# Attention issued in an order computed by a list scheduler, and the gate row applied after w_out

## The chip, the cores and the metric

One core of one Trainium2 chip runs the whole program. The metric is device time in microseconds, the median of the runs. Each core has a matrix engine (TensorE, PE), a vector engine (VectorE, DVE), a scalar engine (ScalarE, ACT), GpSimd (POOL) and a queue engine for transfers (SyncE, SP). Each engine runs its own instructions in the order in which they were issued to it and waits on semaphores for the others.

## What is computed

One transformer block on 1024 tokens of width 1024, batch 1, all in fp32. Cut to what matters here:

```
cond = silu(c)
sh1, sc1, gt1, sh2, sc2, gt2 = split(cond @ w_ada + b_ada, 6)      # "conditioning", 6 x 1024
h    = layer_norm(x) * (1 + sc1) + sh1
aq, ak, av, iq, ik, iw, gq, gk, gv, gr, glr, gate_a, gate_b = split(h @ w_in)
o_a  = sparse attention (8 heads of 64; per query the 256 best keys by an index score)
       logits = q.k / 8 + bias(distance);  p = softmax(logits);  o_a = p @ v
o_b  = gated linear attention, normed                              # 4 heads, 512 columns
merged = sigmoid(gate_a) * (o_a @ w_branch_a) + sigmoid(gate_b) * (o_b @ w_branch_b)
y    = merged @ w_out
x1   = layer_norm(2**0.25 * x + gt1 * y) * g1 + b1
h2   = layer_norm(x1) * (1 + sc2) + sh2
out  = layer_norm(2**0.25 * x1 + gt2 * mixture_of_experts(h2))     # 32 experts, 2 of them per token
```

## The kernel before

The program runs through stages: the first conditioning group (shift and scale 1) and the norm; the projections by w_in with index scores, top-k and the gated linear attention beside them; attention; branch a with the preparation of w_out; the products with w_out with the two norms and the routing; the experts; the last norm. Products that must be exact are made in three passes: an operand is split into a high part (a copy rounded by ACT) and a low part (the difference, by DVE or POOL), and `mm3` adds high x high, high x low and low x high.

**Attention** (lines 883 to 1003) goes by four pairs of heads `p`, each with eight blocks of 128 queries `i`. By the top-k, `acc[i]` already holds 0 or -1e30 per key. `scores(p, i)` lets POOL add mask and distance bias for the last 256 keys (`amb`), PE make the logits of both heads (`asp`, L904, contraction 64, each head on its half of the rows, n = 128(i+1) keys in chunks of at most 512, high and low parts of q and k in three passes), DVE add the mask and find the row's extreme in one custom operation (L908), ACT take the exponential with its row sum (L914), and DVE divide by the sum (L915, L916). Each head has a logits tile of its own, of four in all. `pv(p, u, P)`, for two query blocks at a time, transposes the shares by PE (`atp`, L932 and L933), copies them from PSUM by ACT or DVE in a fixed pattern (`DCOPY`, L936 and L938), multiplies by v (`aop`, L941, each head on its half of the columns), and splits the result into high and low parts (L944, L945). The values of one step are taken up after the scores of the next.

Between these steps `pump(FILL[u])` draws fillers from two generators: `ada_late`, the other two conditioning groups, and `branch_b`, the sixteen sums of o_b by w_branch_b (L124 to L126 by `mm3`, then L981 by DVE, which multiplies with the sigmoid of the gate). A conditioning group has eight steps of k; `ada_step` (L182 to L190) loads two tiles of 128x1024, half a megabyte each, and issues two matmuls on each (L189), each on 32 columns of the array:

```
for i in range(2):
    w = pool.tile([128, 1024], F32, name="wada", bufs=bufs)
    SY.dma_start(w, A["w_ada"][0, k * 128:(k + 1) * 128, c0:c0 + 1024])
    for q in range(2):
        PE.matmul(ps[32 * j:32 * j + 32], crep[:, k, :], w[:, q * 512:(q + 1) * 512], ...)
```

The first stage issues the same operation as four matmuls of 256 columns on one tile (L237). The attention stage stands outside of the manual schedules; the framework places its instructions, and the trace has them in an order that differs from the text (a conditioning step can stand between the transposes of one block).

**Branch a** (L1049 to L1084) goes by eight column blocks f: three-pass products of o_a with w_branch_a (`yps`), multiplied by gate a (L1064) and added to branch b (L1065) on DVE, then split (L1071 on ACT, L1072 on DVE) into `pg`. In the same loop a block of w_out is loaded, multiplied by the gate row gt1 (L1079, on POOL for the f in `GTP`, else on DVE, 128x512 at a time), and split (L1081 on ACT; L1082 on POOL for the f in `GTL`, else on DVE).

**The products** (L1381 to L1413) multiply the merged rows with w_out for each of eight tiles of 128 tokens, in four quarters; PSUM has five buffers `yps` for them and for transposes. `residual` (L1245) adds 2**0.25 x on DVE (L1248) and takes the statistics, and the norms, transposes, routing logits and routing of the tiles before are woven in. x tiles lie in five buffers `lx`.

Of the kernel before, what the change touches and what calls it, by code (L numbers as in the profile page):

```python
# [10 lines left out]
F32 = mybir.dt.float32  # L11
# [5 lines left out]
OP = mybir.AluOpType  # L17
# [39 lines left out]
GTL = (3, 7)  # L57
GTP = (0, 1, 2, 4, 5, 6)
FET = {0: 2, 4: 2, 5: 3, 6: 1, 7: 2}
FILL = (3, 2, 2, 1)  # L60
# [5 lines left out]
DCOPY = (1, 4)  # L66
ASB = 4
# [21 lines left out]
def _bucket_onehot():  # L89
# [8 lines left out]
    return np.ascontiguousarray(oh[:, ::-1])  # L98


@with_exitstack
def block_kernel(ctx, tc, A, out, dbg=None, stop=99):
# [78 lines left out]

    def ada_step(g, k, ps, pool, bufs):  # L182
        for i in range(2):
            w = pool.tile([128, 1024], F32, name="wada", bufs=bufs)
            c0 = g * 2048 + i * 1024
            SY.dma_start(w, A["w_ada"][0, k * 128:(k + 1) * 128, c0:c0 + 1024])
            for q in range(2):
                j = 2 * i + q
                PE.matmul(ps[32 * j:32 * j + 32], crep[:, k, :], w[:, q * 512:(q + 1) * 512],  # L189
                          start=(k == 0), stop=(k == KT - 1), tile_position=(0, 32 * j), skip_group_check=True)  # L190
# [581 lines left out]
    def load_pair(p):  # L772
        for f0, n in ((p * 128, "q"), (512 + p * 128, "k")):
            r = AP_[1].tile([128, S], F32, name="araw", bufs=2)
            SY.dma_start(r, dqk[f0:f0 + 128])
            hi, lo = pair_parts(p, n)
            SC.activation(hi, r, AF.Copy)
            GP.tensor_tensor(lo, r, hi.bitcast(F32), op=OP.subtract)

# [73 lines left out]
    fillers = []  # L853

    def pump(budget):
        while budget > 0 and fillers:
            try:
                budget -= next(fillers[0])
            except StopIteration:
                fillers.pop(0)  # L860

# [21 lines left out]
    def scores(p, i):  # L883

        n = (i + 1) * 128
        (qh, ql), (kh, kl) = QK[p, "q"], QK[p, "k"]
        tk = slice(i * 128, i * 128 + 128)
        f = max(0, n - 256)
        mbs, Ps, mxs = [], [], []
        for s in range(2):  # L890
            mb = apw.tile([128, 256], F32, name="amb")[:, :n - f]
            GP.tensor_tensor(mb, acc[i][:, f:], tb[:, 2 * p + s, 256 - (n - f):], op=OP.add)
            mbs.append(mb)
            Ps.append(apw.tile([128, S], F32, name="aP", bufs=8)[:, :n])
            mxs.append(small.tile([128, 5], F32, name="amx", bufs=8))
# [833 lines left out]
```

## Time and profile before

| | us |
|---|---|
| median of 3 runs (1466.23 to 1469.11) | 1466.5 |
| the profiled execution | 1464.93 |
| its span, first to last instruction | 1463.1 |
| PE busy | 1356.0 (93%) |
| DVE busy | 1166.0 (80%) |
| ACT busy | 729.3 (50%) |
| POOL busy | 499.9 (34%) |

The profile is one execution. The page has the busy time of each engine; the windows give it for a stretch of time, all or for one tile or line; the timeline lists instructions in order of time; the lines group instructions by line and shape. A busy PE is not one at its peak: matmuls are pipelined, so the step from one start to the next is the time that one costs, and the length shown with it is more.

### The profile page before, as it was taken

The page shows a single profiled execution, that of the slowest core. Times are in us where ns is not written, and L with a number is a line of the kernel's source. Part 1 is how long each engine was busy: PE and PEld are TensorE (multiplying, and loading weights), DVE is VectorE, ACT ScalarE, POOL GpSimd, SP SyncE. Part 2 cuts the span into 40 slices and gives each one's busy share as a digit, 9 for nine tenths or more (in the row PEclk, how much of TensorE's full clock was granted, in tenths as well). Part 3 has the DMA queues.
Part 4 walks back from the last instruction along what each step waited for, and adds up shares of the span by engine and source line. Part 5 has one row for each costly group of instructions (what it writes and reads, how often), then busy time and mean ns, then how long its engine had stood idle before and what let it go on. Part 6 is the DMA issues. An engine that isn't in the chain of part 4 may idle for free. (4 is left out here: it accounts for less than half of the span.)

```text
span 1463.1 us, 21360 instructions
## 1 busy us (share of the span) xinstructions
PE 1356.0 (93%) x7535; PEld 1058.7 (72%) x7535; DVE 1166.0 (80%) x2126; ACT 729.3 (50%) x1312; POOL 499.9 (34%) x502
## 2 busy tenths in 40 slices
PE   4988999999999999998999998799969999999975
PEld 2566788887888788983446666599957888888842
DVE  5649998988987899936656656867779999999957
ACT  2456775443243313125544543322327888888934
POOL 2466422374246422144334323521131222222114
PEclk9999999999999999999999999999968999999998
DMA  9454422112211232108555336766349999999965
GB/s 292 149 153 144 144 68 70 59 37 80 77 40 40 85 109 88 58 1 247 185 167 158 108 107 195 232 220 231 130 141 333 379 380 377 376 341 362 368 250 201
DMA packets 135679, 262.69 MB, mean 180 GB/s; under 512 B 20912, under 2 KB 71400, under 8 KB 135568
## 3 DMA queue, kind: packets, MB, share of 16 engines
q1 hardware_dynamic: 124112, 242.13, 48.4%
q0 software_dynamic: 9216, 16.80, 3.1%
q10 hardware_dynamic: 2240, 2.36, 0.5%
q8 instruction: 60, 0.98, 0.3%
q14 instruction: 51, 0.42, 0.1%
HBM read 229.61 MB, written 48.39 MB: 190 GB/s over the span
## 5 line engine op out<-in xcount | busy, mean ns | idle before, releaser
L1357 DVE TENSOR_TENSOR elo<-pg,ehi 128x1024 fp32r<-128x1024 f32 x188 | 219.1, 1220 | 17.5 <-ACT ehi L1352 9.3
L124 PE MATMUL pj<-hTh,whi 128*128 128x512 f32 (+1 forms) x528 | 210.9, 400 | 0.0
L125 PE MATMUL pj<-hTl,whi 128*128 128x512 f32 (+1 forms) x528 | 207.3, 393 | 1.9 <-DVE hTl L267 1.2
L126 PE MATMUL pj<-hTh,wlo 128*128 128x512 f32 (+1 forms) x528 | 207.2, 392 | 0.0
L1352 ACT ACTIVATE ehi<-pg 128x1024 fp32r<-128x1024 f32 x192 | 190.1, 1075 | 1.1 <-PE eph L126 1.1
L791 POOL TENSOR_TENSOR wlo<-raw,whi 128x512 fp32r<-128x512 f32 x84 | 111.8, 1344 | 207.3 <-ACT whi L790 196.3
L485 DVE MATCH_REPLACE8 acc<-m,acc 128x1024 f32<-128x1024 f32 (+2 forms) x192 | 167.4, 881 | 0.0
L482 DVE MAX8 m<-acc 128x8 f32<-128x1024 f32 (+2 forms) x192 | 162.6, 885 | 0.0
L464 DVE SCALAR_TENSOR_TENSOR acc<-ixr,iwt,acc 128x128 f32<-128x128 f32 (+3 forms) x120 | 127.2, 1115 | 13.9 <-ACT ixr L457 13.3
L124 PEld LDWEIGHTS pj<-hTh,whi 128*128 128x128 f32 (+1 forms) x528 | 98.7, 187 | 22.7 <-issue 1.7
L125 PEld LDWEIGHTS pj<-hTl,whi 128*128 128x128 f32 (+1 forms) x528 | 98.8, 187 | 22.5 <-DVE hTl L267 2.7
L126 PEld LDWEIGHTS pj<-hTh,wlo 128*128 128x128 f32 (+1 forms) x528 | 98.6, 187 | 22.8 <-issue 0.6
L124 PE MATMUL pj<-whi,hTh 128*128 128x256 f32 x384 | 111.8, 291 | 0.0
L125 PE MATMUL pj<-wlo,hTh 128*128 128x256 f32 x384 | 108.6, 283 | 0.0
L126 PE MATMUL pj<-whi,hTl 128*128 128x256 f32 x384 | 108.5, 283 | 0.0
L124 PE MATMUL eph<-ehi,xh 128*128 128x512 f32 x256 | 105.4, 412 | 0.0
L125 PE MATMUL eph<-elo,xh 128*128 128x512 f32 x256 | 102.7, 401 | 1.1 <-DVE elo L1362 1.1
L126 PE MATMUL eph<-ehi,xl 128*128 128x512 f32 x256 | 102.7, 401 | 0.0
L457 ACT ACTIVATE ixr<-ips 128x128 f32<-128x128 f32 (+7 forms) x128 | 80.3, 656 | 44.4 <-DVE acc L464 21.1
L1376 POOL DMA_INDIRECT xg<-dh,gidx x32 | 34.0, 1063 | 161.7 <-PE etp L1472 148.5
L124 PEld LDWEIGHTS pj<-whi,hTh 128*128 128x128 f32 x384 | 73.4, 191 | 6.9 <-issue 5.5
L124 PE MATMUL yps<-whi,pg 128*128 128x256 f32 x256 | 75.7, 296 | 2.2 <-ACT pg L1071 2.2
(322 smaller groups left out, 3272.1 us busy)
## 6 DMA issues: line engine op xcount, KB each, us to landing
pg<-in_w_exp_gate_dram SPq DMA_DIRECT2D x64, 512.0 KB
pg<-in_w_exp_up_dram SPq DMA_DIRECT2D x64, 512.0 KB
pg<-in_w_exp_down_dram SPq DMA_DIRECT2D x32, 1024.0 KB
wada<-in_w_ada_dram SPq DMA_DIRECT2D x48, 512.0 KB
raw<-in_w_in_dram SPq DMA_DIRECT2D x20, 1024.0 KB
sraw<-diq SPq DMA_DIRECT2D x68, 128.0 KB
dgate<-gate SPq DMA_DIRECT2D x32, 256.0 KB
gb<-dgate SPq DMA_DIRECT2D x32, 256.0 KB
```

What stands on the lines that cost most here:

```text
L124: PE.matmul(ps, ah, bh, start=first, stop=False)
L125: PE.matmul(ps, ah, bl, start=False, stop=False)
L126: PE.matmul(ps, al, bh, start=False, stop=last)
L457: SC.activation(r, ps, AF.Relu)
L464: V.scalar_tensor_tensor(acc[i], r, sc, acc[i], op0=OP.mult, op1=OP.add)
L482: V.max(m, acc[i])
L485: V.match_replace(acc[i], m, acc[i], -3.0e38)
L791: GP.tensor_tensor(lo[:, k:k + 2], raw[:, k:k + 2], hi[:, k:k + 2].bitcast(F32), op=OP.subtract)
L1352: SC.activation(h3, src, AF.Copy)
L1357: V.tensor_tensor(*args, op=OP.subtract)
L1376: GP.indirect_dma_start(out=x, out_offset=None, in_=dh2, in_offset=bass.IndirectOffsetOnAxis(ap=gi, axis=0), bounds_check=S - 1, oob_is_er ...
```

## The change

In attention a class `Order` takes every step of the stage with its engine (or a choice of ACT and DVE), a modelled time, the steps that it comes after, and the buffers that it takes and gives back. It is run when the program is built: again and again it takes, of the steps that may go, the one with the least start time plus a rank of its kind (`RANK`), and at the end emits all by start time, under a manual schedule for PE, ACT, DVE and POOL. A switch between kinds of PE work is modelled with 0.25 us, a megabyte of conditioning weights with 3.0 us and 2.0 us of lag.

The logits of both heads are one PSUM tile of two banks (`asp`, two of them) and one step. The copies from PSUM are made by ACT or DVE as the scheduler finds. A conditioning step loads 128x2048 at once and issues its four matmuls together. The eight bias loads of both groups are issued ahead of the order. Branch b's o_b parts lie in the conditioning's two buffers.

The gate row gt1 no longer multiplies w_out; `residual` multiplies the product with it on DVE. Of the low parts of w_out DVE makes those of the odd f, POOL those of the even f. `lx` has four buffers, and a tile `ly` is added.

```diff
-GTL = (3, 7)
-GTP = (0, 1, 2, 4, 5, 6)
+GTV = (1, 3, 5, 7)
-FILL = (3, 2, 2, 1)
+RANK = {"Q": 0.94, "R": -22.18, "E": 1.01, "N": 0.11, "T": 1.04, "C": -19.89, "A": 0.98, "H": -49.53, "L": -12.89, "D": 1.04,
+        "B": 0.96, "Z": -18.85, "Wh": 0.27, "Oh": 0.3, "Ol": -62.38, "pair": -3.46, "M": -1.4}
-DCOPY = (1, 4)
-ASB = 4
+class Order:
+    LATENCY, CHANGE = 0.15, 0.25
...
+    def start_of(self, name, free, done, mode):
+        engines, time, _, after, takes, _, m, rank, _ = self.todo[name]
+        if any(a not in done for a in after):
+            return None
+        at = max([done[a] for a in after], default=0.0)
+        for r in takes:
+            n = len(self.taken[r])
+            if n >= self.room[r]:
+                if n - self.room[r] not in self.given[r]:
+                    return None
+                at = max(at, self.given[r][n - self.room[r]])
+        best = None
+        for e, t in zip(engines, time if isinstance(time, tuple) else (time,) * len(engines)):
+            st = max(at, free.get(e, 0.0)) + (self.CHANGE if m and m != mode else 0.0)
+            best = min(best or (st, e, t), (st, e, t), key=lambda x: x[0] + x[2])
+        return (best[0] + rank, *best)
...
+        while self.todo:
+            found = {n: s for n in self.todo if (s := self.start_of(n, free, done, mode))}
+            name = min(found, key=lambda n: found[n][0])
...
-            ps = [app.tile([128, 512], F32, name="asp", bufs=ASB)[:, :e - c] for s in range(2)]
+        ps = T_["asp", p, i, c] = app.tile([128, 2, 512], F32, name="asp", bufs=2)
...
+    def ada_load(g, k):
+        T_["wada", g, k] = aq1.tile([128, 2048], F32, name="wada", bufs=2)
+        SY.dma_start(T_["wada", g, k], A["w_ada"][0, k * 128:(k + 1) * 128, g * 2048:(g + 1) * 2048])
+    def ada_step(g, k):
...
+        for j in range(4):
+            PE.matmul(T_["ada", g][32 * j:32 * j + 32], crep[:, k, :], w[:, j * 512:(j + 1) * 512],
+                      start=(k == 0), stop=(k == KT - 1), tile_position=(0, 32 * j), skip_group_check=True)
...
+                od.add(("Q", p, i, c), TE, 3 * (e - c) * 0.445e-3 + 0.1, run(logits_, p, i, c, e), after, ["asp"],
+                       [("qk", (p, x)) for x in "qk"] if last else [], "q")
...
+            od.add(("Dd", g, k), DMA, 3.0, run(ada_load, g, k), takes=["wada"], lag=2.0)
+            od.add(("D", g, k), TE, 0.9, run(ada_step, g, k), [("Dd", g, k)] + ([("D", g, k - 1)] if k else []),
+                   [] if k else ["adaps"], [("wada", ("Dd", g, k))], "d")
...
+    with tc.manual_schedule(engines=ALL):
+        od.write()
...
-        gt1 = bw.tile([128, D], F32, name="gt1", bufs=1)
-        SC.dma_start(gt1, dada[0:1].to_broadcast([128, D]))
...
-                (GP if f in GTP else V).tensor_tensor(
-                    raw[:, ks], raw[:, ks], gt1[:, None, f * 128:(f + 1) * 128].to_broadcast([128, GTK, 128]), op=OP.mult)
-                (GP if f in GTL else V).tensor_tensor(wol[u][:, ks, cs], raw[:, ks], woh[u][:, ks, cs].bitcast(F32),
+                (V if f in GTV else GP).tensor_tensor(wol[u][:, ks, cs], raw[:, ks], woh[u][:, ks, cs].bitcast(F32),
...
-        V.scalar_tensor_tensor(z[:, sl], z[:, sl], ALPHA, prod.pop((t, half)), op0=OP.mult, op1=OP.add)
+        y = lw.tile([128, 512], F32, name="ly", bufs=1)
+        V.tensor_tensor(y, prod.pop((t, half)), rows["gt1"][:, sl], op=OP.mult)
+        V.scalar_tensor_tensor(z[:, sl], z[:, sl], ALPHA, y, op0=OP.mult, op1=OP.add)
...
-    for n, src in (("g1", A["ln1_g"][0:1]), ("b1", A["ln1_b"][0:1]), ("sc2", dada[2:3]), ("sh2", dada[1:2])):
+    for n, src in (("gt1", dada[0:1]), ("g1", A["ln1_g"][0:1]), ("b1", A["ln1_b"][0:1]), ("sc2", dada[2:3]), ("sh2", dada[1:2])):
```

## Rows read from the trace of the kernel before

**Rows 1.** The page, section 1: busy us, share of the span, instructions.

```profile
PE 1356.0 (93%) x7535; PEld 1058.7 (72%) x7535; DVE 1166.0 (80%) x2126; ACT 729.3 (50%) x1312; POOL 499.9 (34%) x502
```

**Rows 2.** Windows: length, busy PE, PEld, DVE, ACT, POOL; clock, DMA, GB/s.

```profile
659.50:881.50 222.00, 208.61 (x1218) 114.88 (x1216) 139.37 (x446) 109.07 (x237) 81.88 (x89) 1.00 0.51 160
881.50:953.00 71.50, 56.94 (x236) 44.16 (x237) 57.31 (x90) 24.84 (x62) 34.82 (x27) 0.93 0.71 221
953.00:1068.00 115.00, 112.70 (x910) 111.20 (x908) 83.23 (x230) 26.91 (x65) 20.94 (x28) 0.96 0.54 189
```

**Rows 3.** Windows by tile: asp, atp, aop, adaps; then L189 alone.

```profile
659.50:881.50 222.00, 50.53 (x288) 27.47 (x288) 57.63 (x128) 1.00 0.51 160
659.50:881.50 222.00, 45.02 (x288) 30.91 (x288) 12.64 (x20) 31.06 (x60) 1.00 0.51 160
659.50:881.50 222.00, 44.26 (x320) 18.53 (x320) 6.28 (x15) 6.10 (x16) 1.00 0.51 160
659.50:881.50 222.00, 86.48 (x320) 38.53 (x320) 12.42 (x18) 1.00 0.51 160
660.00:885.00 225.00, 33.67 (x128) 4.61 (x128) 1.00 0.52 161
```

**Rows 4.** Timeline, last pair of heads, PE: start, us, line, out<-in, shape, count.

```profile
859.78 0.50 PE L904 MATMUL asp<-akh,aqh 64*128 64x512 f32 x1 [0.17 <-DVE amx L908]
...
861.28 0.33 PE L933 MATMUL atp<-ident,aP 128*128 128x128 f32 x1
...
861.76 0.54 PE L904 MATMUL asp<-akh,aqh 64*128 64x512 f32 x2
...
862.10 0.45 PE L904 MATMUL asp<-akh,aql 64*128 64x512 f32 x2
...
862.33 0.44 PE L904 MATMUL asp<-akl,aqh 64*128 64x512 f32 x2
...
862.70 0.33 PE L932 MATMUL atp<-ident,aP 128*128 128x128 f32 x1
...
862.87 0.27 PE L933 MATMUL atp<-ident,aP 128*128 128x128 f32 x1
...
862.98 0.27 PE L932 MATMUL atp<-ident,aP 128*128 128x128 f32 x1
...
863.43 0.39 PE L125 MATMUL adaps<-obl,whi 128*128 128x512 f32 x1
...
863.66 0.39 PE L126 MATMUL adaps<-obh,wlo 128*128 128x512 f32 x1
```

**Rows 5.** Timeline, PE: two weighted steps and a switch; three and one.

```profile
867.01 1.08 PE L941 MATMUL aop<-ath,vc 128*64 128x256 f32 x8
...
868.02 0.33 PE L932 MATMUL atp<-ident,aP 128*128 128x128 f32 x1
...
873.08 1.52 PE L941 MATMUL aop<-ath,vc 128*64 128x256 f32 x12
...
874.53 0.33 PE L932 MATMUL atp<-ident,aP 128*128 128x128 f32 x1
```

**Rows 6.** Timeline, PE: conditioning in first stage (fours), attention (twos).

```profile
25.75 2.46 PE L237 MATMUL adaps<-wada,crep 128*32 128x256 f32 x40
...
663.98 1.05 PE L189 MATMUL adaps<-wada,crep 128*32 128x512 f32 x4 [1.49 <-DMA wada<-in_w_ada_dram]
```

**Rows 7.** Waits of PE: line, releaser: us in total, times, longest.

```profile
PE adaps L189 <- DMA wada<-in_w_ada_dram: 6.1, 6, 1.5
```

**Rows 8.** Lines, branch a: shapes, count | busy us, mean ns | idle before.

```profile
L1064 DVE TENSOR_TENSOR ga<-yps,ga 128x512 f32<-128x512 f32 x16 | 10.9, 681 | 5.5 <-DMA ga<-dgate 5.5
...
L1072 DVE TENSOR_TENSOR pg<-ga,pg 128x128 fp32r<-128x128 f32 x32 | 15.8, 547 | 0.6 <-ACT pg L1071 0.6
...
L1082 DVE TENSOR_TENSOR wlo<-raw,whi 128x512 fp32r<-128x512 f32 x12 | 12.6, 1049 | 5.1 <-ACT whi L1081 4.8
...
L1079 POOL TENSOR_TENSOR raw<-raw,gt 128x512 f32<-128x512 f32 x12 | 17.4, 1472 | 23.4 <-DMA raw<-in_w_out_dram 21.9 <-DVE pg L1072 1.5
```

More of the change, by code (lines that the diff above doesn't have):

```diff
@@ L98, in _bucket_onehot, with __init__, add, write @@
     return np.ascontiguousarray(oh[:, ::-1])
+class Order:
+    LATENCY, CHANGE = 0.15, 0.25
+    def __init__(self, **room):
+        self.room, self.todo, self.taken, self.given = room, {}, {r: {} for r in room}, {r: {} for r in room}
+    def add(self, name, engines, time, do, after=(), takes=(), gives=(), mode=None, lag=0.0):
+        rank = RANK.get(name[0] if isinstance(name[0], str) else "pair", 0.0)
+        self.todo[name] = (engines, time, do, after, takes, gives, mode, rank, lag)
+    def start_of(self, name, free, done, mode):
[14 more added lines that the diff above has]
+        return (best[0] + rank, *best)
+    def write(self):
+        free, done, mode, out = {}, {}, None, []
+        while self.todo:
+            found = {n: s for n in self.todo if (s := self.start_of(n, free, done, mode))}
+            name = min(found, key=lambda n: found[n][0])
+            _, st, e, t = found[name]
+            _, _, do, _, takes, gives, m, _, lag = self.todo.pop(name)
+            free[e] = st + t
+            done[name] = st + t + self.LATENCY + lag
+            mode = m or mode
+            for r in takes:
+                self.taken[r][name] = len(self.taken[r])
+            for r, who in gives:
+                self.given[r][self.taken[r][who]] = done[name]
+            out.append((st, len(out), e, name, do))
+        self.end = max(free.values())
+        self.out = out = sorted(out, key=lambda x: x[:2])
+        for _, _, e, _, do in out:
+            do(e)
 @with_exitstack
@@ L886, in scores, with logits_ @@
+    def logits_(p, i, c, e):
         (qh, ql), (kh, kl) = QK[p, "q"], QK[p, "k"]
         tk = slice(i * 128, i * 128 + 128)
-        f = max(0, n - 256)
-        mbs, Ps, mxs = [], [], []
-        for s in range(2):
[L891 to L895, printed above, removed]
@@ new lines, in block_kernel @@
+    for p in range(4):
+        for x in "qk":
+            if p < 2:
+                od.taken["qk"][p, x] = len(od.taken["qk"])
+                continue
+            od.add(("Ld", p, x), DMA, 1.6, run(pair_load, p, x), takes=["araw"], lag=2.0)
+            od.add((p, x), ACT, 1.05, run(pair_high, p, x), [("Ld", p, x)], ["qk"])
+            od.add(("Ll", p, x), POOL, 2.4, run(pair_low, p, x), [(p, x)], gives=[("araw", ("Ld", p, x))])
+    od.room["qk"] = 4
+    for g in (1, 2):
+        T_["bada", g] = ada_bias(g, aq1)
+        for k in range(KT):
+            od.add(("Dd", g, k), DMA, 3.0, run(ada_load, g, k), takes=["wada"], lag=2.0)
+            od.add(("D", g, k), TE, 0.9, run(ada_step, g, k), [("Dd", g, k)] + ([("D", g, k - 1)] if k else []),
+                   [] if k else ["adaps"], [("wada", ("Dd", g, k))], "d")
+        od.add(("F", g), DVE, 0.69, run(ada_out, g), [("D", g, KT - 1)], gives=[("adaps", ("D", g, 0))])
```

293 lines of the change are left out of this document (177 added, 116 removed).

## The prediction

> **What bounds the kernel now.** I read the page first: TensorE (PE) is busy 93% of the span [rows 1], so a shorter attention stage can only come from PE doing its work in less time or from its few idle microseconds. Then the windows by stage [rows 2], which give the three stretches that the change touches. In attention (222.0 us) PE is busy 208.61, VectorE (DVE) 139.37, ScalarE (ACT) 109.07 and GpSimd (POOL) 81.88; DMA stands at 0.51, the granted clock at 1.00. PE is the bound; the reader should see that no other engine is near. In the stretch of branch a and the w_out weights (71.5 us) PE is busy only 56.94 and DVE 57.31, with POOL 34.82; neither is full, since they wait for each other's parts of one weight block. In the products (115.0 us) PE is full again (112.70), DVE has 83.23.
>
> Third, the attention stretch tile by tile [rows 3]. PE's busy time there is logits (asp) 50.53, transposes (atp) 45.02, weighted values (aop) 44.26, and adaps 86.48, of which the conditioning (L189) is 33.67 and branch b the other 52.8. These overlap a little, so their sum is above 208.61. Fourth, the timeline, for what the same steps take when they run undisturbed [rows 4 to 6].
>
> **The change part by part: attention.** What the list scheduler may save is PE time that is not array work, so I price every kind of step at its undisturbed spacing.
>
> Logits: a chunk needs six matmuls, two heads by three products. At 859.78 the heads run one after the other and six matmuls of 512 columns take 1.50 us until the next transpose; at 861.76 the heads are adjacent, the six take 0.94, and one pair follows the other after 0.23 [rows 4]. So two heads side by side cost what one costs, and leaving the run costs 0.94 - 0.69 = 0.25. The change gives both heads one PSUM tile, so they cannot be separated. Columns: 4608 per pair of heads (128 to 1024 in steps of 128), times 4 pairs, times 3 products, at 0.23 per 512: 24.8 us, against 50.53 now.
>
> Transposes: 288 at 0.11 (862.87 to 862.98) [rows 4], 31.7. Weighted values: three steps and a switch take 1.45, two and a switch 1.01 [rows 5], so a full step is 0.44 and a switch 0.13; 64 full steps and 16 half ones are 31.7. Branch b: 192 matmuls at 0.23 (863.43 to 863.66) [rows 4], 44.2.
>
> Conditioning: the kernel before issues two matmuls per 0.5 MB tile; each such pair takes 1.05 [rows 6], and 32 pairs make the 33.67 of [rows 3]. In the first stage the same operation is issued in fours of 256 columns: 40 records, which are five groups of four with two records each, take 2.46 [rows 6], 0.49 a group, so 0.98 for 512 columns. Four by column group cost what two cost; 16 groups are 15.7, a saving of 18.
>
> The trace shows this side by side in the five groups. The Trainium skill, TensorE: Matmul & The Clock Gate, in its table of measured speedups under packing small matmuls, has three column tiles 2.38 times as fast and not three times. By that ratio a group would be about a quarter dearer, and the saving 4 us smaller.
>
> Sum of array work: 24.8 + 31.7 + 31.7 + 44.2 + 15.7 = 148.1. Switches between kinds: I estimate 44 runs of logits at 0.25, 65 of weighted values at 0.13, 90 of transposes and branch b at 0.06 (862.70 to 862.87 is 0.17 where 0.11 is plain) and 16 of conditioning at 0.07: 26 us. The count is my choice; the code allows at most 48, 80, 144 and 16, 32 us, and longer runs bring it to 15. Idle: 13.4 now (222.0 - 208.61). I keep that and add 2, because a whole 1 MB must land before a group of four starts and PE already waited 6.1 us for the halves [rows 7]; what is queued behind such a wait is every logit and transpose, and DVE waits for those. Bounds 8 and 30. Attention becomes 148 + 26 + 15 = 189, against 222: **-33**, bounds 171 and 210, so -51 and -12 (fewest switches with 8 idle, most with 30). Cover: DVE's 139 and ACT's 109 still fit in 189, POOL's 82 too. The copies now go to whichever of ACT and DVE the scheduler thinks is free first, which moves time between two engines with room.
>
> The Trainium skill, TensorEngine Tiling, key properties, says that a change of tiling mode drains TensorE. Here the exits cost 0.06 to 0.25; if each of 215 switches cost the dearest, 54 us would replace the 26 and the saving would be 5.
>
> Moved steps: the eight bias DMAs of the conditioning are all issued on ACT's queue before the order begins, four earlier than now; the pair loads, branch-b loads, stores and gate loads stay on SP's queue, in the scheduler's order. SP is nearly empty and holds none of PE's operands but those loads; I cost this at nothing, up to 2 us if a load sits behind a store. Branch b's inputs now take over the two buffers of the conditioning, so it has to wait for the last group, and its second half for the first; attention itself covers both waits. The w_branch_a weights can no longer be made ahead among the attention's last steps on ACT and POOL, if the written order is closed there: 1.5 us once, between 0 and 3.
>
> **Gate row, in branch a.** The multiplication of w_out by the gate leaves this stretch: 12 operations on POOL (17.4 us), 4 on DVE. Of the 16 low parts DVE keeps 8 instead of 12, POOL has 8 instead of 4. DVE: minus 4 x 0.68 (priced as the 128x512 product of L1064), minus 4 x 1.05: -6.9. POOL: -17.4 + 4 x 1.47 = -11.5 [rows 8]. DVE is also slowed by POOL: 32 operations of 128x128 take 0.55 each here, a low part of 128x512 takes 1.05 where L1064 of the same size, with one operand in PSUM, takes 0.68. That excess is about 32 x 0.33 + 12 x 0.37 = 15 us (0.22 for a quiet 128x128 is my estimate, a little over a quarter of 0.68), against POOL's 34.82, so 0.43 per microsecond; 11.5 less of POOL gives 5 back. Together 12 of DVE's 57.31. PE's own work here is 192 x 0.23 = 44 and DMA is at 0.71, so the next bounds lie close; I take 10 of the 12, and less the 1.5 above **-8.5**, bounds -15 and 0.
>
> Where POOL and DVE meet the trace has 0.43 lost per microsecond. The Trainium skill, SBUF — State Buffer, two separate sides, has the pair of ports they share as a lock held for a whole instruction. Were every POOL microsecond lost to DVE, the 5 would be 11.5, and this stretch some 6 better.
>
> **Gate row, in the products.** Added: 16 multiplications of 128x512 from PSUM on DVE, at 0.68 [rows 8] 10.9 us; the residual itself stays. DVE goes from 83 to 94 of 115, so PE stays the bound and covers 14 of the 16. The last one is exposed, 0.7, and what queues ahead of it costs up to 1.4. The gate row (0.5 MB) is loaded third, behind two x tiles; the first residual waits for it, some 2.8 us at 189 GB/s [rows 2], behind which the other rows wait 2.8 too; five PSUM buffers let PE run on. One x buffer fewer: the load of tile t+2 waits for the transposes of t-2, nearly two tiles ahead of its use, and the expert fetches behind it on SP wait with it. I take **+2.5**, bounds 0.7 and 6.
>
> **Sum:** -33 - 8.5 + 2.5 = -39. The profiled execution took 1464.93 (span 1463.1), the median is 1466.5; from the median, 1427.5.
>
> **The rivals.**
> A. The fillers run out early. Conditioning and branch b are taken as soon as PE is free for them, and are gone after some 130 us with half of attention left; then DVE sets the pace with at most 139.37 / 4 = 35 us per pair, 130 + 70 = 200 instead of 189. For it: every kind has nearly the same rank. Against: DVE's 35 still contains its share of the fillers. 1438, chance 0.16.
> B. PE in order on late groups, the slower side. The order is written for 3 us a megabyte and 2 us of lag. PE stands at the first matmul of a group, with every logit behind it, and DVE and ACT run dry. The loss passes the 39 us gained from 2.4 us of lateness per group, 16 groups; at 3 us late it is 48, so 1475. For it: 6.1 us of such waits now, the longest 1.5 [rows 7]. Against: DMA at 0.51 [rows 2]. Chance 0.05.
> C. The order does not do what it says: switches stay as many and as dear as now, and only the pairing and the fours count. PE's busy time falls by the 18 of the fours and about 8 of the logits, but dependencies take half: -13 - 8.5 + 2.5, 1447. Chance 0.13.
> D. Branch a is held by DMA or PE and gives nothing, attention as forecast: 1436. Chance 0.16.
>
> **How the numbers follow.** The forecast, 1427.5, has 0.5; A 0.16, D 0.16, C 0.13, B 0.05. The low end takes the better bounds that can meet: -45 in attention, -14, +1: 1408. The high end takes in C with a little: 1450. A measurement of this kernel tells about 0.2% (3 us) from no change; no case but B comes near it, and a B of just 2.4 us lateness is the same. Faster 0.94, same 0.02, slower 0.04.
>
> **What would show it.** Right: asp's busy time in attention near 30, L189's near 16, attention near 189 us with PE still over 90% busy, no L1079, branch a near 62, a new DVE line of 16 at 0.68. Wrong: waits of PE for the conditioning's DMA above 15 us; DVE over 90% in the second half of attention; asp still above 45; a later end of the products by more than 6 us.

## The result and the profile after

The changed kernel takes 1426.9 us (median of 4 runs, 1423.66 to 1432.59) against 1467.8 for the kernel before (4 runs, 1466.23 to 1475.18): a ratio of 0.9717, 95% interval 0.9689 to 0.9744. The forecast was 1427.5. The profiled execution of the changed kernel is the slowest of its four, 1432.59 us (span 1430.5).

The page, section 1, of the changed kernel (busy us, share of the span, instructions); it answers to [rows 1]:

```profile
PE 1323.1 (92%) x7535; PEld 1060.2 (74%) x7535; DVE 1163.0 (81%) x2118; ACT 734.8 (51%) x1328; POOL 486.2 (34%) x494
```

PE is busy 33 us less with the same 7535 instructions, POOL 14 us less, DVE and ACT about as long as before. To compare stages I cut both traces at the same instructions: the first matmul of attention, of branch a, of the products, and the last matmul of the products. Windows of the kernel before, then of the changed one (length, busy time of PE, PEld, DVE, ACT and POOL, granted clock, DMA share, GB/s):

```profile
660.50:882.00 221.50, 208.34 (x1217) 114.89 (x1217) 139.80 (x447) 108.47 (x236) 81.30 (x88) 1.00 0.51 160
882.00:944.50 62.50, 51.28 (x193) 38.90 (x194) 48.62 (x72) 21.18 (x51) 30.53 (x20) 0.92 0.73 223
944.50:1066.30 121.80, 117.70 (x947) 115.89 (x946) 90.32 (x241) 30.18 (x73) 25.23 (x35) 0.96 0.55 193
```

```profile
663.40:852.00 188.60, 174.60 (x1216) 113.43 (x1216) 134.62 (x431) 114.43 (x252) 80.52 (x89) 0.95 0.54 183
852.00:905.00 53.00, 46.77 (x192) 36.88 (x193) 41.46 (x65) 20.57 (x51) 18.76 (x14) 0.97 0.82 253
905.00:1030.80 125.80, 120.71 (x947) 118.85 (x946) 98.73 (x253) 29.70 (x73) 22.57 (x35) 0.93 0.55 195
```

Attention gave 32.9 us, nearly all of it PE's busy time; branch a gave 9.5; the products took 4.0 back. The rest of this profile is 5.8 longer in code that the change leaves alone: attention starts 2.9 later, and the stretch behind the products takes 399.7 in place of 396.8 (it lies between 397 and 400 in all kernels below). The windows of attention by tile (asp, atp, aop, adaps, then the conditioning's matmuls alone), as in [rows 3]:

```profile
663.40:852.00 188.60, 36.92 (x288) 23.97 (x288) 57.08 (x128) 0.95 0.54 183
663.40:852.00 188.60, 44.38 (x288) 34.65 (x288) 2.41 (x4) 40.20 (x76) 0.95 0.54 183
663.40:852.00 188.60, 38.11 (x320) 20.53 (x320) 6.70 (x16) 6.06 (x16) 0.95 0.54 183
663.40:852.00 188.60, 75.61 (x320) 35.50 (x320) 12.36 (x18) 0.95 0.54 183
663.40:852.00 188.60, 18.95 (x128) 2.96 (x128) 0.95 0.54 183
```

The granted clock is no longer 1.00 throughout: 0.95 here, with 0.50 (1.2 of 2.4 GHz) from 667.7 to 678.0, soon after the start, and from 701.9 to 708.7. The profile of the kernel before has neither stretch.

### The profile page after: what moved, and what is told of

Same layout as the page of the kernel before. It is cut to its first block, busy times and chain, and to the rows that moved or that the text cites. A ratio compares the mean times of both kernels' runs of the same rounds, so it can differ in the third digit from the quotient of the medians.

```text
span 1430.5 us, 21328 instructions
## 1 busy us (share of the span) xinstructions
PE 1323.1 (92%) x7535; PEld 1060.2 (74%) x7535; DVE 1163.0 (81%) x2118; ACT 734.8 (51%) x1328; POOL 486.2 (34%) x494
## 5 line engine op out<-in xcount | busy, mean ns | idle before, releaser
L1512 DVE TENSOR_TENSOR elo<-pg,ehi 128x1024 fp32r<-128x1024 f32 x188 | 219.1, 1220 | 17.5 <-ACT ehi L1507 13.4
L823 POOL TENSOR_TENSOR wlo<-raw,whi 128x512 fp32r<-128x512 f32 x84 | 112.0, 1347 | 209.5 <-ACT whi L822 200.5
L497 ACT ACTIVATE ixr<-ips 128x128 f32<-128x128 f32 (+7 forms) x128 | 80.4, 656 | 44.3 <-DVE acc L504 21.6
```

Source lines behind the costliest of these rows:

```text
L497: SC.activation(r, ps, AF.Relu)
L823: GP.tensor_tensor(lo[:, k:k + 2], raw[:, k:k + 2], hi[:, k:k + 2].bitcast(F32), op=OP.subtract)
L1512: V.tensor_tensor(*args, op=OP.subtract)
```

## The experiments

Each stage below goes from first matmul to first matmul in the one profiled execution (products: to their last matmul). Each ratio is against runs of the kernel before that were made beside the runs of the variant. Kernels with the changed kernel's attention order and one logits tile scatter from 184.0 to 188.7 in attention, so a difference of under some 4 us in attention in one profile is not read as an effect. With the gate row in the residual and loaded as in the changed kernel, branch a scatters from 51.8 to 54.6 behind a written order, the products from 123.2 to 129.5.

| kernel | median us | ratio to before, 95% | attention | branch a | products |
|---|---|---|---|---|---|
| before | 1467.8 | 1 | 221.5 | 62.5 | 121.8 |
| changed | 1426.9 | 0.9689 to 0.9744 | 188.7 | 53.0 | 125.7 |
| e1 attention only | 1427.05 | 0.9672 to 0.9732 | 184.7 | 58.6 | 121.6 |
| e2 gate only | 1464.31 | 0.9931 to 0.9964 | 226.0 | 49.2 | 124.7 |
| e3 heads apart | 1428.31 | 0.9677 to 0.9767 | 185.8 | 52.9 | 128.6 |
| e10 heads apart, two tiles | 1432.46 | 0.9739 to 0.9777 | 187.5 | 52.2 | 129.5 |
| e7 one tile only | 1467.12 | 0.9979 to 1.0001 | 222.9 | 62.4 | 124.6 |
| e6 twos | 1451.03 | 0.9854 to 0.9902 | 209.5 | 54.6 | 124.8 |
| e4 text order | 1668.66 | 1.1341 to 1.1379 | 435.7 | 51.8 | 123.2 |
| e12 planner | 1447.96 | 0.9819 to 0.9883 | 210.6 | 49.8 | 127.4 |
| e9 no ranks | 1456.75 | 0.9872 to 0.9933 | 212.7 | 53.4 | 128.4 |
| e5 bias late | 1428.17 | 0.9693 to 0.9753 | 184.6 | 54.3 | 125.6 |
| e11 row early | 1422.91 | 0.9650 to 0.9731 | 184.0 | 57.4 | 116.2 |
| e13 four edits | 1430.24 | 0.9686 to 0.9750 | 191.3 | 57.9 | 118.1 |

### What is the order worth? e4, e12, e9

e4 takes the changed kernel's steps and emits them under the manual schedule in the order of the old text. `emit` runs a step by name, and copies from PSUM go by the old fixed pattern, not by the scheduler's choice. The added lines are condensed here.

```diff
-        od.write()
+        for p in range(4):
+            for u in range(4):
+                for i in (2 * u, 2 * u + 1): ...   # M, then Q and R by chunk, E, N
+                if last: values(*last)             # T, C, A for each j; H, L
+                last = (p, u)
+                for _ in range((3, 2, 2, 1)[u]):
+                    next(fl)                       # one conditioning step or one branch-b sum
```

> The changed kernel's steps (one tile for both heads, conditioning by fours, the same buffers), but written in the order of the kernel before's text: logits of a tile, the values of the tile pair before, then three, two, two and one filler steps. The scheduler is not asked. Theory (the saved work of TensorE becomes time only if other kinds are interleaved finely): about half of the 33 us of attention is lost, to waits of PE for DVE's and ACT's results behind a row of the same kind; attention about 205 to 210, total about 1443. Rival C of the prediction turned round (the fours and the one tile are the whole gain, the order none of it): attention within 5 us of the changed kernel's 189, total within 6 us of it.

It took 1668.66 us, attention 435.7. Waits of PE in attention (line, releaser: us in total, times, longest) and the window of attention in e4:

```profile
PE aop L991 <- ACT ath L982: 89.7, 60, 5.7
PE aop L991 <- DVE ath L980: 30.2, 20, 8.3
```

```profile
661.60:1097.20 435.60, 281.34 (x1216) 146.37 (x1216) 139.47 (x447) 112.04 (x237) 77.09 (x89) 0.65 0.26 86
```

Each of the 80 weighted steps waits 1.5 us on average for its own copy, since nothing stands between transpose and weighted step. PE is left idle a third of the time and is granted 0.65. Its busy time grows too, from 174.60 to 281.34 for the same 1216 records, somewhat more than the clock alone would make it (174.60 x 0.95 / 0.65 = 255). Both theories were far off. But this order is not what the kernel before ran: there the planner moved the instructions. So e12 gives the same text to the planner:

```diff
-    with tc.manual_schedule(engines=ALL):
+    if True:
         fl = fillers()
```

> The steps of the run e4 in the same order of the text, but not fixed: as in the kernel before, the planner that orders the rest of the kernel is left to move them. So this is the changed kernel with pairs and fours and without its scheduler. Theory (PE's saved work has to meet an order that feeds it; e7 showed that the pairs alone gave 4.5 us of logits' time and none of the total): PE's busy time falls by the fours' 15 and the pairs' 10 against the kernel before, its waits take half of it, attention 205 to 212, total about 1445. Rival (the planner does as well as the scheduler): attention within 5 us of the changed kernel's.

1447.96 us, attention 210.6: the times that the theory gave, and 1 us from rival C's 1447. The way to them was another: PE's busy time falls by 14 us against the kernel before, not by 25, and its idle time takes 3 of that, not half. So pairs and fours without the scheduler bring 11 us of attention; the written order, with the scheduler's choice of engine for the copies, brings another 22 to 27. Window of e12, the same stretch:

```profile
659.60:870.30 210.70, 194.08 (x1217) 111.31 (x1217) 139.75 (x447) 109.20 (x238) 80.07 (x89) 0.98 0.54 179
```

PE's idle time is 16.6 here and 14.0 in the changed kernel; what the order takes away is busy time, 194.08 against 174.60, for the same matmuls. The order of PE's matmuls says where it goes: from first logit to branch a the kernel before changes between the five kinds of work 244 times, e12 222 times, the changed kernel 169; in runs of logits 63, 50 and 25, of weighted steps 53, 59 and 28. These have the dear exits of [rows 4, 5]. Summed in the traces from each matmul's start to the next one's, without PE's idle time and with time at 0.50 counted half:

| us | steps within a kind | steps that leave a kind |
|---|---|---|
| before | 133.5 | 74.8 (244) |
| e12 | 125.7 | 64.9 (222) |
| changed | 129.3 | 37.6 (169) |

Leaving a kind is what the written order saves, 27 us between e12 and the changed kernel; steps within a kind and the clock take 4 us each back. At the prices that the prediction took from [rows 4, 5] the exits would differ by 10; why a single exit costs more in e12 as well (0.29 against 0.22 on average) is not shown.

e9 keeps the scheduler and sets its ranks to zero:

```diff
-RANK = {"Q": 0.94, "R": -22.18, "E": 1.01, "N": 0.11, "T": 1.04, "C": -19.89, "A": 0.98, ...
+RANK = {
+        }
```

> The changed kernel with all ranks of the list scheduler at zero: among the steps that may run, the one that can start first is written first. Theory (PE is busy 92% of attention; what the order must do is to let some step of PE always be ready, and the ranks only refine that): attention within 6 us of the changed kernel, total 1428 to 1434. Rival (the low ranks of smallest, copies and high parts are what keeps DVE and ACT serving PE first): attention 10 to 25 us longer, with PE's waits for amx and ath above 15 us, total 1440 to 1450.

The rival's mechanism came closer, and its size was exceeded: 1456.75 us, attention 212.7, in the total worse than the planner's order. It has the fewest changes of kind, 125, and PE's busy time is 179.21; its idle time is 33.5, with 19 in waits for amx and ath (row extremes and copied shares), as the rival had it. Windows of the last 52.7 us of attention, e9, then the changed kernel:

```profile
820.70:873.40 52.70, 41.03 (x175) 28.82 (x174) 11.55 (x18) 11.62 (x21) 14.62 (x12) 0.90 0.51 165
```

```profile
799.30:852.00 52.70, 51.08 (x336) 36.49 (x332) 33.95 (x99) 31.38 (x64) 17.55 (x19) 1.00 0.41 128
```

In e9 the attention steps are used up early and branch b's sums stand alone at the end (175 matmul records against 336, DVE at 11.55), where each waits 0.9 us for the multiplication that frees the one buffer:

```profile
PE adaps L174 <- DVE gb L1060: 6.9, 8, 0.9
```

The ranks are worth some 24 to 29 us of attention; few switches alone are not the aim. Which of the ranks does it was not tried.

### What pairs the heads? e7, e3, e10

e7 is the kernel before with one logits tile for both heads:

```diff
-            ps = [app.tile([128, 512], F32, name="asp", bufs=ASB)[:, :e - c] for s in range(2)]
+            pp = app.tile([128, 2, 512], F32, name="asp", bufs=2)
+            ps = [pp[:, s, :e - c] for s in range(2)]
```

> The kernel before with one tile for both heads' logits, nothing else. The program then has 128 of 144 chunks' products side by side, against 98 pairs of 190 rows before. Theory (two heads cost one when their products may start together): the logits' busy time falls from 50.5 to about 40, attention by 8 to 10 us to about 213, total about 1458. Rival (the order of the kernel before waits for DVE instead): asp falls likewise, PE's idle time takes it up, and the total is within 3 us of the kernel before.

The rival's time held: 1467.12 us, ratio 0.9979 to 1.0001. The logits' busy time fell from 50.5 to 46.02, that of the weighted steps rose from 44.3 to 49.30, and PE's idle time stayed at 13.2, so it was not idle time that took the gain up, as the rival had it, but other busy time:

```profile
663.90:886.80 222.90, 209.74 (x1217) 113.43 (x1217) 139.03 (x447) 108.75 (x236) 80.77 (x88) 0.98 0.51 159
663.90:886.80 222.90, 46.02 (x288) 24.79 (x288) 58.59 (x128) 0.98 0.51 159
663.90:886.80 222.90, 49.30 (x320) 19.43 (x320) 6.71 (x16) 6.14 (x16) 0.98 0.51 159
```

These are the window of attention, then asp and aop alone. e3 undoes the pairing in the changed kernel's text:

```diff
-        for j, (q_, k_) in enumerate(((qh, kh), (ql, kh), (qh, kl))):
-            for s in range(2):
+        for s in range(2):
+            for j, (q_, k_) in enumerate(((qh, kh), (ql, kh), (qh, kl))):
```

> The changed kernel with the logits' two loops exchanged: within one step all three products of one head, then all three of the other, so that no two heads stand side by side. Theory (attention is bound by TensorE, and heads side by side run together): the logits' array work doubles from about 25 to 50 us, attention takes about 20 us more than the changed kernel's 190, total about 1447. Rival (VectorE and the chain of dependencies set attention's pace, as DVE's 135 busy of 190 with short waits of PE for amx would suggest): PE's idle time takes it up, and the time is within 6 us of the changed kernel.

The total stayed (1428.31), and not for the rival's reason: the logits were as fast as before, asp 36.82. PE's instructions are three products of one head and then three of the other, and they run side by side all the same. e10 adds a tile of its own for each head:

```diff
-        ps = T_["asp", p, i, c] = app.tile([128, 2, 512], F32, name="asp", bufs=2)
+        ps = T_["asp", p, i, c] = [app.tile([128, 512], F32, name="asp", bufs=4) for _ in range(2)]
```

> The changed kernel with heads apart in the program, as in the run e3, and with a tile of its own for each head. In e3 the program had the heads apart, and the chip ran them side by side all the same (six products of 512 columns in 0.71 us). Theory (the one tile is what pairs them: its release lets both heads start at once, while two tiles come free 0.6 us after each other, as at 859.78 of the kernel before): spacings of 1.5 us for six products are back in part of the chunks, asp above 42 against 37, attention 3 to 10 us longer than in e3. Rival (heads on different rows of the array run side by side whatever the tiles are): asp within 1.5 us of 37, attention within 2 us of e3.

Timeline of PE for the same chunk of 512 columns (start, us, line, out<-in, shapes, count), e3:

```profile
729.40 0.51 PE L932 MATMUL asp<-akh,aqh 64*128 64x512 f32 x2 [0.51 <-DVE amx L950]
729.71 0.43 PE L932 MATMUL asp<-akh,aql 64*128 64x512 f32 x2
729.94 0.43 PE L932 MATMUL asp<-akl,aqh 64*128 64x512 f32 x2
730.30 0.33 PE L972 MATMUL atp<-ident,aP 128*128 128x128 f32 x1
```

and e10:

```profile
731.83 0.39 PE L932 MATMUL asp<-akh,aqh 64*128 64x512 f32 x1
732.06 0.39 PE L932 MATMUL asp<-akh,aql 64*128 64x512 f32 x1
732.30 0.38 PE L932 MATMUL asp<-akl,aqh 64*128 64x512 f32 x1
732.51 0.47 PE L932 MATMUL asp<-akh,aqh 64*128 64x512 f32 x1
732.82 0.38 PE L932 MATMUL asp<-akh,aql 64*128 64x512 f32 x1
733.04 0.39 PE L932 MATMUL asp<-akl,aqh 64*128 64x512 f32 x1
733.37 0.33 PE L972 MATMUL atp<-ident,aP 128*128 128x128 f32 x1
```

DVE's reads that release the two tiles, then the load of the second head's weights, in e10, and a chunk there with both tiles free:

```profile
731.37 0.08 DVE L950 DVE_READ_ACCUMULATOR2_ANT amx<- 128x1 f32 x1
732.28 0.08 DVE L950 DVE_READ_ACCUMULATOR2_ANT amx<- 128x1 f32 x1
732.48 0.18 PEld L932 LDWEIGHTS asp<-akh,aqh 64*128 64x128 f32 x1 [0.23 <-issue]
```

```profile
731.01 0.50 PE L932 MATMUL asp<-akh,aqh 64*128 64x512 f32 x2
```

With one tile both heads wait once and the six products take 0.90; with two, head 0 starts without a wait, head 1's tile comes free 0.91 later, and the six take 1.54, much as the 1.50 of [rows 4]. Where both tiles are free, e10 runs them side by side too. So the theory's mechanism is shown, at a smaller size: asp is 40.40 against 36.82, where above 42 was expected. The time it costs is small: from the chunk before (727.91 and 731.01) to the transpose it is 2.39 us in e3 and 2.36 in e10, since head 0 uses the 0.51 us that e3 waits. Attention's 187.5 is inside the scatter, and the intervals of the two ratios overlap. Counted by starts (two records with the same operands within 0.08 us), 150 of the 288 logits matmuls run side by side in the kernel before, 214 in e7, 206 in e12, 226 in e10, and all of them in the changed kernel and e3. So under the planner the one tile pairs only part of them, and e10 undoes a fifth of the pairing; a written order with no heads side by side was not run.

### The fours: e6

```diff
-        for j in range(4):
+        for j in (2 * t, 2 * t + 1):
...
+            for t in range(2):
+                od.add(("D", g, k, t), TE, 0.9, run(ada_step, g, k, t), ..., "d", 0.0 if t else 1.5)
```

> The changed kernel with each conditioning step written as two steps of two column groups, the second 1.5 us or more behind the first where the scheduler has other work. Theory (four column groups cost what two cost): 16 more groups at about 1 us, conditioning's busy time 33 instead of 19, attention 12 to 15 us longer, total about 1440. Rival (the fours did not carry the gain, since conditioning stands where PE would wait anyway): within 4 us of the changed kernel.

1451.03 us, attention 209.5: the theory's direction, but 21 us longer where 12 to 15 were expected. Lines of the conditioning's matmuls in attention (busy us, mean ns, idle before), e6, then e11, which of the kernels with the fours has the least time at 0.50 in attention:

```profile
L1023 PE MATMUL adaps<-wada,crep 128*32 128x512 f32 x128 | 27.8, 619 | 1.0 <-DMA wada<-in_w_ada_dram 0.9
```

```profile
L1023 PE MATMUL adaps<-wada,crep 128*32 128x512 f32 x128 | 17.5, 632 | 3.7 <-DMA wada<-in_w_ada_dram 3.7
```

The fours themselves are worth 10 us. The rest of the 21 goes with another order: with other steps the scheduler wrote one with 8.78 us of copies on DVE in place of 2.41, PE's waits for DVE's row extreme (amx) are 13.6 us in place of 4.7, and its idle time is 22.8 in place of 14.0. A step cannot be changed in this kernel without changing the order of all others, so e6 does not isolate the fours.

### The gate row: e1, e2, e11

e1 has the new attention and the old gate, e2 the reverse.

```diff
+                (GP if f in GTP else V).tensor_tensor(
+                    raw[:, ks], raw[:, ks], gt1[:, None, f * 128:(f + 1) * 128].to_broadcast([128, GTK, 128]), op=OP.mult)
...
-        V.tensor_tensor(y, prod.pop((t, half)), rows["gt1"][:, sl], op=OP.mult)
```

> The new attention alone; the gate is multiplied into w_out's weights in branch a as in the kernel before. Theory (the parts add up): attention takes about 190 us against 222 and everything behind it is as before, so about 1466.5 - 33 = 1434, some 5 us above the changed kernel. Rival (branch a's end is set by loads that start only with attention's end, so that the gate's work there was hidden): branch a takes 53 here too, and the time is within 2 us of the changed kernel, or below it by the products' +4.

> The old attention with the gate row multiplied on the projection's result. Theory: attention stays at 222 us, branch a (from its first product to the first of the out projection) falls from 62.5 to about 53, the products take 4 us more: about 1461, a ratio of 0.996. Rival (the shorter branch a of the changed kernel comes from the attention's end, where loads and weights were ready earlier): branch a stays above 60, and the time is 1467 or, with the products' +4, above it.

e1 took 1427.05 us, no more than the changed kernel: the time of its rival, but with branch a at 58.6 and not at the rival's 53. e2 took 0.9948 of before, 5 to 10 us less, as its theory said (0.996). So the gate part is worth some 7 us with the old attention and nothing that can be measured with the new one. The window of attention in e1, then those of branch a, e1 and e2:

```profile
661.60:846.30 184.70, 171.64 (x1216) 112.14 (x1217) 134.47 (x431) 114.38 (x252) 80.61 (x89) 0.97 0.55 187
```

```profile
846.30:904.90 58.60, 48.69 (x192) 38.05 (x193) 49.82 (x72) 20.74 (x51) 31.53 (x21) 0.91 0.78 240
```

```profile
889.50:938.70 49.20, 46.58 (x193) 36.93 (x194) 40.24 (x67) 21.17 (x53) 20.58 (x14) 0.97 0.71 219
```

The gate alone takes 13.3 off branch a (62.5 to 49.2). Behind a fixed order the same branch a needs 53.0, in six more kernels 51.8 to 54.6; e12, which has the gate part and no fixed order, 49.8. So the closed order costs 2 to 5 us there. With the gate still on w_out the closed order does not cost but gives 3.9 (e1). Why it differs was not tried. e2's profile also has attention 4.5 longer than before, at a granted clock of 0.97, with code that the edit does not touch.

In the products the kernels with the gate on w_out take 121.6 (e1), 121.8 (before) and 124.6 (e7), those with it in the residual 123.2 to 129.5, so some 4 us more on the whole, and not clear for a single kernel. The first residual on DVE in the changed kernel (timeline):

```profile
920.89 0.69 DVE L1402 TENSOR_TENSOR ly<-yps,rowgt 128x512 f32<-128x512 f32 x1 [7.41 <-DMA rowgt<-dada]
```

e11 puts the row beside w_out's weights and loads it in the middle of branch a:

```diff
+    rows["gt1"] = wo.tile([128, D], F32, name="rowgt1")
...
+            if f == 4:
+                SY.dma_start(rows["gt1"], dada[0:1].to_broadcast([128, D]))
...
-    for n, src in (("gt1", dada[0:1]), ("g1", ...
+    for n, src in (("g1", ...
```

> The changed kernel with its gate row loaded in the middle of branch a, into a buffer beside w_out's weights, in place of the third load behind branch a. Theory (the products take 4 us more because DVE's first residual waits 7.4 us for the gate row): the first gate multiplication starts some 3 us earlier (then held by the first x tile), the products, from their first to their last multiplication, fall from 125.7 to about 122, total about 1424. Rival (the extra 16 DVE operations of 0.68 us lengthen each tile's chain to its logits, on which PE waits near the fifth tile): the products stay within 1 us of 125.7, total within 2 us of the changed kernel.

Timeline of DVE and window of the products in e11:

```profile
906.49 0.69 DVE L1405 TENSOR_TENSOR ly<-yps,rowgt 128x512 f32<-128x512 f32 x1 [1.15 <-PE yps L176]
909.82 0.69 DVE L1406 SCALAR_TENSOR_TENSOR lx<-lx,ly 128x512 f32<-128x512 f32 x1 [2.63 <-DMA lx<-in_x_dram]
```

```profile
900.50:1016.70 116.20, 114.32 (x947) 112.83 (x946) 95.54 (x245) 28.89 (x69) 20.82 (x33) 0.99 0.56 200
```

The products fall to 116.2, further than the theory's 122 and below those of before, and PE's granted clock in them is 0.99 in place of 0.93 (e13, with the same edit: 0.97). Of the 9.5 us, 6.4 are PE's busy time. The nine kernels with the late row have 0.91 to 0.96; but e7, which has no such row in the products, has 0.93 too, so that the late row cost clock is likely and not shown. Branch a takes 57.4, 4 us more than without the row's load in it (e13, with the same edit, 57.9 and 118.1). Branch a and products together are 173.6 and 176.0 in these two, 178.7 to 181.8 in the changed kernel, e3, e5, e6, e9 and e10, and 175.0 and 177.2 in e4 and e12, whose attention ends in another order. In e2, behind the old attention and with the late row, they are 173.9, as low as in e11. The total, 1422.91, is the lowest here, but its interval (0.9650 to 0.9731) overlaps the changed kernel's, so that it beats it is likely and not shown.

### The start of attention: e5, e13

Timeline of ACT at the start of attention in the changed kernel (ACTq: transfers issued on ACT's queue):

```profile
663.34 6.08 ACTq L229 DMA_DIRECT2D bada<-in_b_ada_dram  x7
669.45 1.28 ACT L959 ACT_TABLE_LOAD   x1 [5.48 <-DMA bada<-in_b_ada_dram]
670.75 0.40 ACT L959 ACTIVATE aP<-aP,amx 128x128 f32<-128x128 f32 x1
```

The eight bias transfers hold ACT for 6 us; the first exponential comes 7.4 us after the first logit, 1.9 in the kernel before. e5 moves them to SP's queue and to the sixth step of each group:

```diff
+        if k == 5:
+            T_["bada", g] = ada_bias(g, aq1, SY)
...
-        T_["bada", g] = ada_bias(g, aq1)
```

> The changed kernel with the eight bias DMAs taken off ACT's queue ahead of the order; each group's four are issued on SP's queue at its sixth conditioning load. Theory (they block ACT for 6 us, the first exponential comes some 5.5 us late, and PE runs dry behind it and falls to a granted clock of 0.50): the first exponential comes within 1.5 us of the first logits' last product, attention falls by 4 to 6 us to about 184, total about 1422. Rival (PE's start is held by the masks, made behind the key conversion on POOL, and by the pair loads ahead of the conditioning's): the stage gains under 1.5 us, total within 2 us of the changed kernel.

In e5 the first exponential starts 2.9 us after the first logit:

```profile
666.71 0.40 ACT L959 ACTIVATE aP<-aP,amx 128x128 f32<-128x128 f32 x1 [0.94 <-DVE amx L950]
```

and nothing measurable follows from it: 1428.17 us, with attention, 184.6, inside the scatter. The rival was right about the time. The windows from 668 to 676, the changed kernel, then e5:

```profile
668.00:676.00 8.00, 6.92 (x32) 3.77 (x32) 7.16 (x31) 5.75 (x17) 5.19 (x8) 0.50 1.03 313
```

```profile
668.00:676.00 8.00, 6.89 (x33) 3.27 (x30) 6.98 (x30) 4.20 (x12) 5.72 (x9) 0.50 0.54 227
```

PE has the same work and half the clock in both; before these windows it waited 2.34 us for DVE, and DVE for the masks, which stood on POOL behind the last low part of the keys. e13 takes that low part to DVE and lets the conditioning's loads go ahead of the next pair's, beside the edits of e5 and e11:

```diff
-                GP.tensor_tensor(hl[1][:, sl], gt, hl[0][:, sl].bitcast(F32), op=OP.subtract)
+                (V if (u, m, half) == (2, 1, 1) else GP).tensor_tensor(hl[1][:, sl], gt, ...
...
-            od.add(("Ld", p, x), DMA, 1.6, run(pair_load, p, x), takes=["araw"], lag=2.0)
+            od.add(("Ld", p, x), DMA, 1.6, run(pair_load, p, x), [("D", 1, 1) if p == 2 else (2, x)], ["araw"], lag=2.0)
```

> The changed kernel with four edits: bias DMAs as in e5, gate row as in e11, the last low part of the keys on DVE in place of POOL (so that the first masks don't stand behind it), and the pair loads of the third pair behind the second conditioning step, so that the conditioning's loads go first. Theory (the start of attention at a granted clock of 0.50 comes from PE being idle 2.3 us for DVE, which waited for the masks, with no conditioning yet landed): the first 16 us of attention gain 4 to 6 us, attention 179 to 182, with the row 1418 to 1421. Rival (the start is bound by the 1 MB loads, so PE waits for them wherever the pair loads stand, and their order moves waits elsewhere): attention stays 184 to 186, total 1422 to 1426.

Worse than either: 1430.24, attention 191.3, PE's waits for the conditioning 5.4 us; as the rival had it, the waits moved elsewhere. The clock from 668 to 676 rose to 0.69, and fell to 0.59 from 692 to 700, where PE was busy 5.94 of 8 us. The stretch at 0.50 at the start lasts some 10 us in the changed kernel, e1, e3, e5 and e10, and some 7 in e11, which has no edit there. Nor is it the new order's alone. e2 and e7, with the old attention, have it too; e7:

```profile
666.20:673.00 6.80, 5.63 (x16) 1.38 (x16) 2.98 (x16) 2.61 (x10) 4.44 (x7) 0.50 0.77 267
```

What the low clock at the start costs, and what would remove it, stays open.

## Why the prediction was right, point by point

**The total** was right to 0.6 us. In the profile the three stages came out near their forecasts, -32.9, -9.5 and +4.0. But so near a total is luck in part, since by the other runs two of its parts were off against each other: by e1, attention alone is worth the whole change, 36.8 us of that stage in its profile where 33 were forecast, and the gate part, forecast at -6, is worth 5 to 10 with the old attention (e2) and nothing measurable on top of the new one.

**Attention**, 189: 188.6 in the profiled execution, 184 to 186 in four others with the same steps in the same order (e1, e3, e5, e11). PE's busy time was to be 148 + 26 = 174, and is 174.60; the idle time 15, and is 14.0. But the 26 for switches is right only by chance: 169 changes of kind in place of 215, at the prediction's own prices 25 x 0.25 + 28 x 0.13 + 104 x 0.06 + 12 x 0.07 = 17. The other 9 are about what a granted clock of 0.95 takes from 174.6. The prediction had no term for the clock.

**Pairs and fours.** The sum took each kind of step at its undisturbed spacing, which makes the logits 14.7 cheaper (50.53 less 24.8 and 44 exits at 0.25) and the conditioning 18. Summed from start to start as above, the logits went from 47.0 to 32.8, the conditioning from 31.5 to 15.5, and the other three kinds together lost 11 us; the clock takes back 7.7 and idle time 0.9, which leaves 33. So the sizes were about right. What failed is to count them as gains of these two edits; only its rival C priced the edits without the order, at 13 us of attention. Pairs alone give nothing (e7), the fours are worth 10 in their own busy time (e6), and both together 11 of attention under the planner (e12); the rest is the order's. The sum came out because it priced every kind at its undisturbed spacing, and of the orders tried only the ranked one, with few changes of kind and PE fed, comes near that spacing. The order with neither pairs nor fours was not run. Four groups do cost what two cost, 1.06 to 1.07 for a group of four in e11's timeline at full clock against 1.05 for two of [rows 6]:

```profile
671.89 1.06 PE L1023 MATMUL adaps<-wada,crep 128*32 128x512 f32 x8 [0.39 <-DMA wada<-in_w_ada_dram]
```

The Trainium skill, TensorE: Matmul & The Clock Gate, has three column tiles 2.38 times as fast as one and not three times (measured speedups, under packing small matmuls). No such loss is seen here between two groups and four; one group alone was not run.

**The signs** that were to show it: adaps' conditioning near 16 (17.5 in e11, 18.95 in this profile), PE over 90% (92.6%), waits for the conditioning's transfers under 15 (4.4), a new line of DVE at 0.68 (0.69): right. asp near 30 was wrong, 36.92, by an error of reading: a busy row counts the whole length of the last matmul of a run, 0.39, and the sum counted spacings of 0.23. The four tiles' rows add up to 195 where PE is busy 174.60.

**The rivals.** A did not come, and in e9, where PE ran short, the fillers were left over and not used up. B: 4.4 us of waits. C's price, 1447, is what e12 measured for its condition. D did not come as told, since branch a gave 9.5 us, but its outcome did: with the new attention the gate part gives the total nothing (e1).

**Bias transfers**, costed at nothing up to 2: the cover held, though not because the queue was short. They block ACT for 6 us, and e5 shows that this is hidden by a start that is late anyway.

**Branch a**, -8.5: -9.5. Its terms: the gate alone gives 13.3 (e2), where 10 were taken; closing the order costs 2 to 5, where 1.5 were. The relief of DVE by a shorter POOL was to be 5 us; the splits of 128x128 went from 15.8 in all [rows 8] to 13.3, a low part from 1.05 to 1.09, so it was about 2. In e2, with as little POOL work there (20.7 us, 20.9 in the changed kernel), the splits fell to 9.9, a relief of 6. So the prediction's 0.43 per microsecond of POOL is no fixed rate.

**Products**, +2.5: +4.0, within the bounds. The named mechanism, the row loaded third, is there and was mis-sized: DVE waits 7.4 us for it, not 2.8. The prediction let PE run on through that wait and had no term for the clock; of the 4.0, PE's busy time is 3.0, at a granted clock of 0.93 in place of 0.96. e11 shows that with the row early the stage is 9.5 us shorter, and branch a 4.4 longer.

## What to carry to other kernels

Price a reordering by what each kind of step takes undisturbed, plus a price per change of kind, and do not hand the gain to the single edits: here pairs alone gave nothing, pairs and fours 11 us, and the written order, with the same edits, 22 to 27 more. When work moves to a later stage, its new operand has to be there when that stage begins; with a row that came 7 us late, taking 16 multiplications out of a busy stage gained nothing measurable behind the new attention, and with the row early the two stages together were 3 to 5 us shorter. A written order is tuned as one piece: an edit inside it (twos, ranks, a load moved) rewrites all of it, so compare such kernels by stage and not by the edit.

## What the runs showed of the hardware

- Matmuls on different halves of the rows run side by side even when the program has three of one half ahead of three of the other (e3: six products of 512 columns in 0.90 us). What kept them apart was a wait of their own: with separate tiles, released 0.91 us after each other, the second head's three came behind the first's, 1.54 us (e10).
- Where PE ran short of work its granted clock was lower too, which multiplies the price of a wait: 0.65 over the attention of e4, where PE was busy 281 of 436 us, and 0.90 against 1.00 over the last 52.7 us of attention in e9 (41.0 busy) and the changed kernel (51.1).
- How long DVE takes beside POOL is not set by the amount of POOL's work alone: 32 splits of 128x128 took 0.55 us each beside 34 us of POOL work (before), 0.47 beside 20.9 (changed kernel) and 0.36 beside 20.7 (e2).
